# S5 coefficients once per layer, layer 1's tables during layer 0's last projection, lerp and gates with fewer GpSimd passes, three columns opened together

## The chip, the core and the metric

The kernel runs on one core of a Trainium2 chip. The metric is the device time of one execution in microseconds (us). A core has five engines that run side by side, each with its own in-order queue: TensorE (PE, matmuls; PEld is its weight load), VectorE (DVE), ScalarE (ACT), GpSimd (POOL), and SyncE (SP), which here issues the DMAs. Semaphores between the queues carry the dependences.

## The reference

Two pre-norm residual layers on 512 positions of width 2048. The lines that matter here:

```python
h = rms_norm(x);  p = h @ w_in                       # 2048 -> 6,592 columns, then split:
#  A latent attention   B S5   C RWKV-7   D differential attention   and a gate of width 2048
# B (32 groups of 16 channels, one 64-dim complex state per group), coefficients of a layer only:
mag = exp(dt * lr); ab = mag * (cos(dt * li) + i sin(dt * li)); f = (ab - 1) / (lr + i li)
bb = f * (b_re + i b_im);   h_t = ab * h_(t-1) + bb u_t;   y = Re(c h) + d u   # associative scan
# C: token shift of every one of its 13 column tiles
z = z + (z_prev - z) * mu                            # z_prev is z one position earlier
# all four: mix and project
y = concat(A, B, C, D) * silu(gate);  x = x + y @ w_out
```

A final norm follows the last layer.

## The kernel before

**Matmuls.** Everything is fp32 in three passes of a rounded format: each operand is split into a high and a low part, and `three` (L129 records its matmuls) adds low x high, high x low and high x high. `big` runs one output column of 128 features over 512 positions: it streams the weights in chunks of 128x512 (four k tiles of 128). For each chunk SP loads `raw`, ACT casts it to `wh` (L244), DVE subtracts to get `wl` (L245), and PE runs 12 matmuls of 128x512. The ring holds three chunks. A column of the input projection has 16 k tiles, so 48 matmuls. `XH` and `XL` are the two parts of the input times the norm's gain; the norm's row factor `rxr` is multiplied in when a column leaves PSUM (`evacuate`).

**Order.** PE's order is written by hand: `PE.drive` walks the main program `everything` (input projection, output projection, layer by layer) and lets tasks put in their small matmuls at yields given in us of a nominal clock: `recurrent` (RWKV), `others` (S5, both attentions), and the norm. On the other engines a scheduler sets the order at build time, with a head start for the weight chunks. Each engine then runs its list in order, so a DVE instruction that waits for POOL holds up the `wl` behind it.

**The start.** `everything` begins the first two columns of layer 0 together, while x is loaded: per k tile `absorb` makes XH on ACT and XL on DVE (L453), `sum_sq` the square on ACT and the sum `sqs` on POOL (L461). The third column comes after. Up to five columns may wait in PSUM for the norm's factor.

**S5.** `s5_tables` (L329) runs at the head of `others` in both layers: 128x32 tiles of powers of the state factor `pr`, `pi`, then for each of four quarters q a 332-wide tile of coefficients `sm`, written to DRAM, and a rotation table over 64 positions (`tq`, `tr`, `cs`), whose five 128x512 products and sums run on POOL (L434 to L440). `s5_unit` runs 8 times a layer: it loads `sm` (1,328 bytes for each partition), the table and its input, and first makes on POOL `prs` (L794, signed powers) and then, in 8 steps, a copy L809 and a signed copy L810 of the powers in reverse order. DVE forms `CA` (L802 to L804) and `AB` (L811 to L813) from them.

**Lerp and gates.** `z_tile` (L488) evacuates a RWKV column: `zr` on DVE (L494), the difference with the position before on POOL (L496), and z = difference x mu + zr on DVE (L497). A gate column takes a tanh on ACT, a scale and two products on POOL (L1378 to L1380); `mix` (L1388) splits the result into MH and ML for the output projection. The output projection of layer 0 (`out_proj`) runs 16 columns; each result is also absorbed as layer 1's input.

Of the kernel before, what the change touches and what calls it, by code (L numbers as in the profile page):

```python
# [72 lines left out]
ST = {}  # L73
_c = 0
for _n, _w in (("pr", 36), ("pi", 36), ("m8", 4), ("b1", 64), ("b2", 64), ("c1", 64), ("c2", 64)):
    ST[_n] = (_c, _w)
    _c += _w
NST = _c
# [112 lines left out]
def trunk(ctx, tc, io, KT=16, depth=DEPTH):  # L191
# [137 lines left out]
    def s5_tables(pl, l):  # L329
# [23 lines left out]
        pr = pl.tile([128, 9, 32], F32, name="spr", tag="spr")  # L353
        pi = pl.tile([128, 9, 32], F32, name="spi", tag="spi")
        tp = pl.tile([128, 4, 32], F32, name="stp", tag="stp")
        V.memset(pr[:, 0], 1.0)
        V.memset(pi[:, 0], 0.0)
        V.tensor_tensor(out=pr[:, 1], in0=mag, in1=cs, op=ALU.mult)
        V.tensor_tensor(out=pi[:, 1], in0=mag, in1=sn, op=ALU.mult)
        for n in (1, 2, 4):  # L360
            br = pr[:, n:n + 1].to_broadcast([128, n, 32])
            bi = pi[:, n:n + 1].to_broadcast([128, n, 32])
            cmul(pl, V, pr[:, n + 1:2 * n + 1], pi[:, n + 1:2 * n + 1],
                 pr[:, 1:n + 1], pi[:, 1:n + 1], br, bi, tp[:, :n])
        m8 = t32("m8")
# [29 lines left out]
        for q in range(4):  # L395
            g0 = 8 * q
            yield 4.0
            sm = pl.tile([128, 2, NST], F32, name="ssm", tag="ssm", bufs=2)
# [21 lines left out]
            for o, x, y, op in (("b1", 0, 1, ALU.add), ("b2", 1, 0, ALU.subtract)):  # L420
                V.tensor_tensor(out=w2, in0=bc[:, x], in1=frb, op=ALU.mult)
                V.tensor_tensor(out=w, in0=bc[:, y], in1=fib, op=ALU.mult)
                V.tensor_tensor(out=smv(o), in0=halves(w2), in1=halves(w), op=op)
            V.tensor_copy(out=smv("c1"), in_=halves(bc[:, 2]))
            V.tensor_copy(out=smv("c2"), in_=halves(bc[:, 3]))
            SP.dma_start(out=s5sm[l, q], in_=sm.rearrange("p h n -> p (h n)"))
            yield 4.0
# [337 lines left out]
    def s5_unit(sp, l, e, uD, ysD):  # L765
# [17 lines left out]
        def smv(n):  # L783
            o, w = ST[n]
            return sm[:, o:o + w]

        pr = smv("pr").rearrange("p (j g) -> p g j", g=4)
        pi = smv("pi").rearrange("p (j g) -> p g j", g=4)
        b1, b2, c1, c2 = (smv(n).rearrange("p (g c) -> p g c", c=16) for n in ("b1", "b2", "c1", "c2"))
# [904 lines left out]
```

## Time and profile before

| | |
|---|---|
| median of 3 runs | 2083.63 us (2079.5 to 2087.05) |
| profiled execution | 2085.61 us, its span 2083.8 us |
| PE busy | 1977.2 us, 95% |
| DVE busy | 1328.6 us, 64% |
| ACT busy | 816.1 us, 39% |
| POOL busy | 649.7 us, 31% |
| mean granted PE clock | 0.977 of full |

The profile's times count from the first instruction of the span. A row of the timeline has start, duration, engine, line and operation, the tiles out<-in, and in brackets the idle time of the engine before it with what ended that idle time. A row with a count covers several like instructions, and its duration is of them together. An engine's busy time in a window counts stalls inside an instruction too, so an operation that is slowed by its neighbour shows as a longer one.

### The profile page before, as it was taken

To read this page: it belongs to the slowest core of one execution; us is meant where nothing else is said; L and a number is where in the kernel's file an instruction comes from. 1 tells how busy PE (TensorE), PEld (TensorE's weight loads), DVE (VectorE), ACT (ScalarE), POOL (GpSimd) and SP (SyncE) were. 2 spreads that over 40 slices of the span, in tenths; PEclk is the share of its full clock that TensorE was granted. 3 is DMA by queue.
4 is the path that set the end of the run, shared out by engine and by line. 5 is a ranking of instruction groups with operands and counts; after the bars stand their busy time and mean duration, and the time that the engine had idled before them with its cause. 6 is when DMAs were issued, how large, how long until landed. Compare 5 with 4: busy or idle time off the path is not lost.

```text
span 2083.8 us, 31759 instructions
## 1 busy us (share of the span) xinstructions
PE 1977.2 (95%) x10975; PEld 1601.9 (77%) x10975; DVE 1328.6 (64%) x2750; ACT 816.1 (39%) x1680; POOL 649.7 (31%) x837
## 2 busy tenths in 40 slices
PE   7888899999999989999998998999999998999997
PEld 5666677787878778888876786778787886888887
DVE  7987765656756677644477776656684666765332
...
GB/s 193 127 139 128 118 112 132 166 177 167 152 176 123 145 180 149 145 120 176 157 110 159 108 120 125 116 144 202 141 178 197 121 130 180 129 162 119 137 150 119
DMA packets 231922, 303.77 MB, mean 146 GB/s; under 512 B 78160, under 2 KB 102992, under 8 KB 231760
## 3 DMA queue, kind: packets, MB, share of 16 engines
...
q10 hardware_dynamic: 144, 0.17, 0.0%
HBM read 232.08 MB, written 67.21 MB: 144 GB/s over the span
## 4 chain that ended last, share of the span: by engine, by line
PE 62%; DVE 13%; DMA 10%; issue 6%; POOL 6%; ACT 3%; SPq 1%; DVEq 0%; ACTq 0%; POOLq 0%
PE acc L129 46%; PE pb L129 13%; DVE wl L245 3%; PE pb L133 2%; DMA sm<-s5sm 2%; POOL pis L810 1%; DMA raw<-in_w_out_dram 1%; POOL prs L809 1%; DMA raw<-in_w_in_dram 1%; DMA R<-qkD 1%; DVE XL L453 1%; ACT wh L244 1%; DMA qs<-qrD 1%; DMA gt<-ysD 1%; DMA stg<-gD 0%
## 5 line engine op out<-in xcount | busy, mean ns | idle before, releaser
L129 PE MATMUL acc<-XH,wl 128*128 128x512 f32 x1616 | 671.0, 415 | 61.1 <-DVE wl L245 55.4
L129 PE MATMUL acc<-XL,wh 128*128 128x512 f32 x1616 | 641.9, 397 | 5.4 <-DVE XL L453 5.3
L129 PE MATMUL acc<-XH,wh 128*128 128x512 f32 x1616 | 641.4, 397 | 0.0
L244 ACT CAST wh<-raw 128x512 fp32r<-128x512 f32 (+1 forms) x560 | 342.3, 616 | 609.7 <-PE acc L129 437.9
L245 DVE TENSOR_TENSOR wl<-raw,wh 128x512 fp32r<-128x512 f32 (+1 forms) x560 | 415.7, 745 | 239.0 <-ACT wh L244 236.4
L129 PEld LDWEIGHTS acc<-XH,wl 128*128 128x128 f32 x1616 | 310.1, 192 | 150.3 <-DVE wl L245 73.7
L129 PEld LDWEIGHTS acc<-XH,wh 128*128 128x128 f32 x1616 | 309.2, 191 | 68.3
L129 PEld LDWEIGHTS acc<-XL,wh 128*128 128x128 f32 x1616 | 310.2, 192 | 67.0 <-DVE XL L453 9.6
L129 PE MATMUL acc<-MH,wl 128*128 128x512 f32 x448 | 178.5, 398 | 0.0
L129 PE MATMUL acc<-MH,wh 128*128 128x512 f32 x448 | 175.7, 392 | 0.0
L129 PE MATMUL acc<-ML,wh 128*128 128x512 f32 x448 | 174.5, 389 | 0.0
L461 POOL TENSOR_TENSOR sqs<-sqs,sq 128x512 f32<-128x512 f32 (+1 forms) x47 | 60.6, 1289 | 200.1 <-ACT sq L459 199.6
L683 POOL TENSOR_SCALAR tmp<-SV,ec 64x64 f32<-64x64 f32 x112 | 66.2, 593 | 176.0 <-DVE SV L710 94.6
L129 PEld LDWEIGHTS acc<-MH,wh 128*128 128x128 f32 x448 | 84.1, 188 | 19.3
L129 PEld LDWEIGHTS acc<-ML,wh 128*128 128x128 f32 x448 | 84.2, 188 | 17.3
L129 PEld LDWEIGHTS acc<-MH,wl 128*128 128x128 f32 x448 | 84.3, 188 | 16.8
L1378 POOL TENSOR_SCALAR zd<-zd 128x512 f32<-128x512 f32 x32 | 22.5, 703 | 226.3 <-ACT zd L1377 190.3
L1209 POOL TENSOR_TENSOR sr<-ss,cc 128x1 f32<-128x1 f32 x32 | 18.2, 571 | 147.9 <-DVE ss L1207 108.8
L496 POOL TENSOR_TENSOR zd<-zr 128x512 f32<-128x512 f32 x26 | 35.7, 1372 | 82.7 <-DVE zr L494 79.5
L810 POOL TENSOR_SCALAR pis<-sm,cc 128x4 f32<-128x4 f32 x128 | 58.9, 460 | 0.0
L924 ACT ACTIVATE pt<-pb,nb,fc 128x128 f32<-128x128 f32 (+3 forms) x64 | 39.5, 617 | 41.1 <-DVE nb L923 41.1
L626 DVE TENSOR_TENSOR tmp<-X 64x30 f32<-64x30 f32 (+14 forms) x120 | 41.1, 343 | 15.5 <-DMA T<-K 5.5
...
## 6 DMA issues: line engine op xcount, KB each, us to landing
...
raw<-in_w_out_dram SPq DMA_DIRECT2D x128, 256.0 KB, 3.4
...
```

What stands on the lines that cost most here:

```text
L129: return self.nc.tensor.matmul(out, lhsT=lhsT, rhs=rhs, **kw)
L133: return self.nc.tensor.transpose(out, in_, identity)
L244: A.copy(out=wh[:, :n], in_=raw[:, :n])
L245: V.tensor_sub(out=wl[:, :n], in0=raw[:, :n], in1=wh[:, :n])
L453: V.scalar_tensor_tensor(out=XL[:, k], in0=x, scalar=g, in1=XH[:, k], op0=ALU.mult, op1=ALU.subtract)
L461: G.tensor_tensor(out=sqs, in0=sqs, in1=sq, op=ALU.add)
L496: G.tensor_tensor(out=d, in0=zr[:, 0:S], in1=zr[:, 1:], op=ALU.subtract)
L626: V.tensor_tensor(out=t2, in0=X[:, 0:j, j:j + 1].to_broadcast([64, j, n]), in1=X[:, j:j + 1, j + 1:32].to_broadcast([64, j, n]), op=ALU.mult)
L683: G.tensor_scalar(out=T1[T, h], in0=SVs[s][T, c, h], scalar1=ec[T, h, c:c + 1], scalar2=None, op0=ALU.mult)
L810: G.tensor_scalar(out=pis[:, :, i], in0=pi[:, :, 7 - i], scalar1=C("sg"), scalar2=None, op0=ALU.mult)
L924: A.activation(out=pt, in_=ps[:, 0:n], func=AF.Exp, scale=fcol[:, qb:qb + 1], bias=nb, accum_out=sm)
L1378: G.tensor_scalar(out=th, in0=th, scalar1=0.5, scalar2=0.5, op0=ALU.mult, op1=ALU.add)
```

## The change

1. **S5 coefficients.** Once per layer one DVE and 16 small ACT instructions put the signed powers, the reversed ones and m8 into one tile `pw` of 35 values for each group (1,120 values a partition), stored as `s5pw`; b goes to `s5b`, c is read straight from the input. A unit loads three pieces (`pw` 560 bytes, `b` 512 bytes, `c` two times 256 bytes for each partition) in place of `sm`, and its 17 POOL instructions are gone.
2. **Tables.** The copies into `sm` are gone, the five 128x512 passes a quarter move from POOL to DVE, the POOL power is cut into four pieces, and layer 1's tables become a task of layer 0's output projection, which ends only when they are made.
3. **Lerp and gates.** The lerp is zr x (1 - mu) on ACT, then one DVE instruction; a gate needs one DVE and one POOL pass after the tanh, and `mix` multiplies by one half.
4. **Start.** Three columns are opened together, the squares are summed on DVE there, and six columns may wait for the norm.

```diff
-    def s5_tables(pl, l):
+    def s5_tables(pl, l, pace):
...
+        a, b = PW["pr"]
+        V.tensor_scalar(out=pw[:, :, a:b], in0=pr, scalar1=C("sg"), scalar2=-1.0, op0=ALU.mult, op1=ALU.mult)
+        for i in range(8):
+            A.copy(out=pw[:, :, PW["rr"][0] + i], in_=pr[:, :, 7 - i])
+            A.activation(out=pw[:, :, PW["ri"][0] + i], in_=pi[:, :, 7 - i], func=AF.Copy, scale=C("sg"))
...
+        SP.dma_start(out=s5pw[l], in_=pw)
+        yield pace
...
-            for n, x in (("pr", pr), ("pi", pi)):
-                for h in range(2):
-                    V.tensor_copy(out=smv(n)[:, h].rearrange("p (j g) -> p j g", g=4),
-                                  in_=x[:, :, g0 + 4 * h:g0 + 4 * h + 4])
-            V.tensor_copy(out=smv("m8"), in_=m8[:, g0:g0 + 8].rearrange("p (h g) -> p h g", g=4))
...
-            G.tensor_tensor(out=tq, in0=qb, in1=hb, op=ALU.mult)
+            V.tensor_tensor(out=tq, in0=qb, in1=hb, op=ALU.mult)
             V.tensor_scalar(out=tr, in0=tq, scalar1=MAGIC, scalar2=MAGIC, op0=ALU.add, op1=ALU.subtract)
-            G.tensor_tensor(out=tq, in0=tq, in1=tr, op=ALU.subtract)
-            G.tensor_tensor(out=tr, in0=qb, in1=lb, op=ALU.mult)
-            G.tensor_tensor(out=tq, in0=tq, in1=tr, op=ALU.add)
+            V.tensor_tensor(out=tq, in0=tq, in1=tr, op=ALU.subtract)
+            yield pace
+            V.tensor_tensor(out=tr, in0=qb, in1=lb, op=ALU.mult)
+            V.tensor_tensor(out=tq, in0=tq, in1=tr, op=ALU.add)
...
     def z_tile(ps, mu, m1, rxr, out):
-        G.tensor_tensor(out=d, in0=zr[:, 0:S], in1=zr[:, 1:], op=ALU.subtract)
-        V.scalar_tensor_tensor(out=out, in0=d, scalar=mu, in1=zr[:, 1:], op0=ALU.mult, op1=ALU.add)
+        A.activation(out=d, in_=zr[:, 1:], func=AF.Copy, scale=m1)
+        V.scalar_tensor_tensor(out=out, in0=zr[:, 0:S], scalar=mu, in1=d, op0=ALU.mult, op1=ALU.add)
...
-        sm = sp.tile([128, NST], F32, name="sm", tag="sm", bufs=2)
-        SP.dma_start(out=sm, in_=s5sm[l, t, :, hf * NST:(hf + 1) * NST])
+        pw = sp.tile([128, 4, NPW], F32, name="pw", tag="pw", bufs=2)
+        SP.dma_start(out=pw, in_=s5pw[l, :, 4 * e:4 * e + 4])
+        bb = sp.tile([128, 4, 4, 16], F32, name="bb", tag="bb", bufs=2)
+        SP.dma_start(out=bb[:, 0:2].rearrange("p a g c -> p a (g c)"), in_=s5b[l, t, :, hf])
+        SP.dma_start(out=bb[:, 2:4].rearrange("p a g c -> p a (g c)"),
+                     in_=io["s5bc"][l, :, 2:4, 64 * e:64 * e + 64])
...
-        G.tensor_scalar(out=prs, in0=pr, scalar1=C("sg"), scalar2=-1.0, op0=ALU.mult, op1=ALU.mult)
...
-        for i in range(8):
-            G.tensor_copy(out=prs[:, :, i], in_=pr[:, :, 7 - i])
-            G.tensor_scalar(out=pis[:, :, i], in0=pi[:, :, 7 - i], scalar1=C("sg"), scalar2=None, op0=ALU.mult)
-        V.tensor_tensor(out=AB, in0=bj(prs[:, :, 0:8]), in1=bc(b1, 8), op=ALU.mult)
+        V.tensor_tensor(out=AB, in0=bj(rr), in1=bc(b1, 8), op=ALU.mult)
...
-                G.tensor_scalar(out=th, in0=th, scalar1=0.5, scalar2=0.5, op0=ALU.mult, op1=ALU.add)
+                V.scalar_tensor_tensor(out=g, in0=th, scalar=1.0, in1=g, op0=ALU.add, op1=ALU.mult)
                 G.tensor_tensor(out=g, in0=g, in1=y, op=ALU.mult)
-                G.tensor_tensor(out=g, in0=g, in1=th, op=ALU.mult)
...
+            PE.spawn(tables(l + 1), 1)
             for m in range(KT):
...
+            while (l + 1, "tab") not in PE.done:
+                yield False
             PE.spawn(norm_task(l + 1, sqs), -1)
...
-        begun = [acc(), acc()]
+        begun = [acc(), acc(), pb()]
...
-                    absorb(st, k0 + j, x[:, j], pvts[0], sqs)
-            yield from big([io["w_in"][0, i] for i in range(2)], KT, XH, XL, begun, st, (8, 4), inputs)
+                    absorb(st, k0 + j, x[:, j], pvts[0], sqs, V)
+            yield from big([io["w_in"][0, i] for i in range(3)], KT, XH, XL, begun, st, (9, 6), inputs)
```

Three places show how the engines' lists move. First DVE around the first S5 units of layer 0, before; `prs` and `pis` come from POOL, `sm` from a DMA, `m` is the scan's factor.

```order
L803 TENSOR_TENSOR W<-sm 128x576 [waits DMAHW6_49]
L846 COPY m_1994<-sm 128x256 [waits DMAHW3_49]
L802 TENSOR_TENSOR CA<-prs,sm 128x576 [waits DMAHW2_49,DMAHW3_49,DVE_49,Pool_49]
L847 MEMSET m_1994 128x4 [waits DVE_49]
L804 TENSOR_TENSOR CA<-CA,W 128x576 [waits DVE_49]
L245 TENSOR_TENSOR wl<-raw,wh 128x512 [waits DMAHW1_49,Activation_49]
L811 TENSOR_TENSOR AB<-prs_1690,sm 128x512 [waits Pool_49]
L812 TENSOR_TENSOR W<-pis,sm 128x4x128 [waits Pool_49]
L803 TENSOR_TENSOR W<-sm 128x576 [waits DMAHW2_49,DVE_49]
L813 TENSOR_TENSOR AB<-AB,W 128x512 [waits DVE_49]
L245 TENSOR_TENSOR wl<-raw,wh 128x512 [waits DMAHW5_49,Activation_49]
```

The same place now; `pw` and `bb` are what the three loads bring.

```order
L836 COPY m_1820<-pw 128x256 [waits DMAHW7_49]
L801 TENSOR_TENSOR AB<-pw,bb 128x512 [waits DMAHW0_49]
L837 MEMSET m_1820 128x4 [waits DVE_49]
L243 TENSOR_TENSOR wl<-raw,wh 128x512 [waits DMAHW3_49,Activation_49]
L796 TENSOR_TENSOR CA<-pw,bb 128x576 [waits DMAHW4_49,DMAHW6_49,DMAHW2_49,DMAHW1_49]
L797 TENSOR_TENSOR W<-pw,bb 128x576
L802 TENSOR_TENSOR W<-pw,bb 128x4x128
L801 TENSOR_TENSOR AB<-pw,bb 128x512 [waits DMAHW6_49,DMAHW5_49]
L798 TENSOR_TENSOR CA<-CA,W 128x576 [waits DVE_49]
L243 TENSOR_TENSOR wl<-raw,wh 128x512 [waits Activation_49]
```

The waits for POOL are gone, and the products wait for DMAs alone. Second, SP's list of DMAs at the same place, before.

```order
L776 DMA sm<-s5sm 128x332
L778 DMA tab<-s5tab 128x2x256 [waits PE_49]
L242 DMA raw<-in_w_in_dram 128x512 [waits DMAHW0_49,DVE_49]
L781 DMA U_1678<-uD_348 128x256 [waits DMAHW1_49]
L776 DMA sm<-s5sm 128x332 [waits DMAHW2_49]
L778 DMA tab<-s5tab 128x2x256 [waits DMAHW3_49,Pool_49]
```

And now:

```order
L774 DMA pw<-s5pw 128x140
L776 DMA bb<-s5b 128x128 [waits DMAHW0_49,PE_49]
L777 DMA bb<-in_s5bc_dram 128x2x64 [waits DMAHW1_49]
L240 DMA raw<-in_w_in_dram 128x512 [waits DMAHW2_49,DVE_49]
L780 DMA tab<-s5tab 128x2x256 [waits DMAHW3_49]
L783 DMA U_1613<-uD_422 128x256 [waits DMAHW4_49]
L774 DMA pw<-s5pw 128x140 [waits DMAHW5_49]
L776 DMA bb<-s5b 128x128 [waits DMAHW6_49]
L777 DMA bb<-in_s5bc_dram 128x2x64 [waits DMAHW7_49]
```

Each unit has two more DMAs ahead of the weight chunks that follow. Third, DVE in the first columns of layer 0's output projection, before; `xo` is a finished column.

```order
L1457 TENSOR_TENSOR xo<-acc,xo 128x512 [waits DMAHW3_49,PE_49]
L245 TENSOR_TENSOR wl<-raw,wh 128x512 [waits DMAHW3_49,Activation_49]
L453 SCALAR_TENSOR_TENSOR XL<-xo,pvt,XH 128x512 [waits Activation_49]
L1457 TENSOR_TENSOR xo<-acc,xo 128x512 [waits DMAHW7_49,DMAHW5_49,PE_49]
L245 TENSOR_TENSOR wl<-raw,wh 128x512 [waits DMAHW4_49,Activation_49]
L453 SCALAR_TENSOR_TENSOR XL<-xo,pvt,XH 128x512 [waits Activation_49]
L245 TENSOR_TENSOR wl<-raw,wh 128x512 [waits DMAHW6_49,Activation_49]
```

And now, with the rotation table of layer 1 (`tq`, `tr`, `cs`):

```order
L243 TENSOR_TENSOR wl<-raw,wh 128x512 [waits DMAHW2_49,Activation_49]
L451 SCALAR_TENSOR_TENSOR XL<-xo,pvt,XH 128x512 [waits Activation_49]
L441 TENSOR_SCALAR cs_9854<-cs_9854,cc 128x512 [waits Activation_49]
L431 TENSOR_TENSOR tq<-cc,sthi 128x512 [waits DVE_49,Activation_49]
L441 TENSOR_SCALAR cs_10060<-cs_10060,cc 128x512 [waits Activation_49]
L431 TENSOR_TENSOR tq<-cc,sthi 128x512 [waits DVE_49,Activation_49]
L243 TENSOR_TENSOR wl<-raw,wh 128x512 [waits DMAHW3_49,Activation_49]
L432 TENSOR_SCALAR tr<-tq 128x512 [waits DVE_49]
L298 TENSOR_SCALAR cs_9854<-cs_9854 128x512 [waits Activation_49]
L298 TENSOR_SCALAR cs_10060<-cs_10060 128x512 [waits Activation_49]
L432 TENSOR_SCALAR tr<-tq 128x512 [waits DVE_49]
L243 TENSOR_TENSOR wl<-raw,wh 128x512 [waits DMAHW6_49,Activation_49]
```

In this piece four table instructions and more stand between two `wl`; before, they stood in layer 1's input projection. From the first table instruction to the last, this list has 26 `wl`.

## Rows read from the trace of the kernel before

**Rows 1.** The page's busy times, shares of the span and instruction counts.

```profile
PE 1977.2 (95%) x10975; PEld 1601.9 (77%) x10975; DVE 1328.6 (64%) x2750; ACT 816.1 (39%) x1680; POOL 649.7 (31%) x837
```

**Rows 2.** PE's waits: engine, line, what it waited for; us, times, longest.

```profile
PE acc L129 <- DVE wl L245: 55.4, 33, 5.6
PE pb L129 <- DVE BK L586: 6.9, 3, 5.9
...
PE acc L129 <- DVE zr L494: 5.1, 1, 5.1
```

**Rows 3.** Busy us (and instructions) of each engine by window, PEclk, DMA share, GB/s.

```profile
6.00:42.00 36.00, 27.35 (x103) 17.98 (x102) 33.05 (x29) 24.09 (x43) 22.77 (x19) 1.00 0.59 209
...
60.00:180.00 120.00, 100.22 (x441) 78.86 (x440) 105.34 (x204) 44.57 (x73) 69.21 (x82) 0.90 0.44 139
220.00:310.00 90.00, 80.50 (x515) 64.89 (x513) 65.28 (x142) 29.75 (x69) 41.36 (x91) 0.89 0.39 116
...
920.00:1060.00 140.00, 140.00 (x617) 115.06 (x617) 62.12 (x94) 53.11 (x86) 25.97 (x25) 1.00 0.51 157
1080.00:1160.00 80.00, 63.84 (x260) 49.46 (x260) 66.48 (x124) 28.36 (x45) 58.93 (x71) 0.87 0.38 128
1240.00:1360.00 120.00, 110.17 (x847) 87.53 (x846) 77.81 (x167) 42.82 (x107) 63.51 (x148) 0.97 0.40 118
```

**Rows 4.** Timeline of the start, and the first matmul of the third column.

```profile
6.99 0.50 PE L129 MATMUL acc<-XH,wl 128*128 128x512 f32 x1 [0.42 <-ACT XH L452]
...
15.54 1.30 POOL L461 TENSOR_TENSOR sqs<-sqs,sq 128x512 f32<-128x512 f32 x1 [0.44 <-ACT sq L459]
15.57 5.87 DVE L453 SCALAR_TENSOR_TENSOR XL<-x,pvt,XH 128x512 fp32r<-128x512 f32 x4
...
23.66 0.74 DVE L453 SCALAR_TENSOR_TENSOR XL<-x,pvt,XH 128x512 fp32r<-128x512 f32 x1
...
41.17 0.39 PE L129 MATMUL pb<-XH,wl 128*128 128x512 f32 x1
```

**Rows 5.** Line L245 over the whole run: ns of one, min/median/max.

```profile
L245 DVE TENSOR_TENSOR wl<-raw,wh x560: 411/691/1781, 6.1 to 2016.2; 128x512 fp32r<-128x512 f32 x184, 128x256 fp32r<-128x256 f32 x3
```

**Rows 6.** Timeline of DVE in the tables of layer 0.

```profile
92.21 0.41 DVE L435 TENSOR_SCALAR tr<-tq 128x512 f32<-128x512 f32 x1
...
92.94 0.28 DVE L423 TENSOR_TENSOR ssm<-sw,sw 128x128 f32<-128x128 f32 x1
```

**Rows 7.** POOL and ACT groups by line: busy us, mean ns, idle before and its releasers.

```profile
L810 POOL TENSOR_SCALAR pis<-sm,cc 128x4 f32<-128x4 f32 x128 | 58.9, 460 | 0.0
...
L809 POOL COPY prs<-sm 128x4 f32<-128x4 f32 x128 | 36.3, 284 | 0.0
L496 POOL TENSOR_TENSOR zd<-zr 128x512 f32<-128x512 f32 x26 | 35.7, 1372 | 82.7 <-DVE zr L494 79.5 <-DVE sfi L384 3.2
...
L434 POOL TENSOR_TENSOR tq<-cc,sthi 128x512 f32<-128x512 f32 x8 | 13.2, 1653 | 4.7 <-ACT cs L298 3.7 <-DVE sthi L393 1.0
```

**Rows 8.** Timeline of two S5 units of layer 0.

```profile
165.30 0.96 POOL L794 TENSOR_SCALAR prs<-sm,cc 128x36 f32<-128x36 f32 x1
...
171.88 0.69 DVE L811 TENSOR_TENSOR AB<-prs,sm 128x512 f32<-128x512 f32 x1 [2.02 <-POOL prs L809]
...
174.38 1.66 DVE L245 TENSOR_TENSOR wl<-raw,wh 128x512 fp32r<-128x512 f32 x1
...
176.10 0.79 PE L129 MATMUL acc<-XH,wl 128*128 128x512 f32 x1 [5.59 <-DVE wl L245]
...
242.41 0.69 DVE L811 TENSOR_TENSOR AB<-prs,sm 128x512 f32<-128x512 f32 x1 [2.89 <-POOL prs L809]
```

**Rows 9.** Timeline of the first S5 units of layer 1.

```profile
1138.33 0.76 DVE L803 TENSOR_TENSOR W<-sm 128x576 f32<-128x576 f32 x1 [3.58 <-DMA sm<-s5sm]
...
1149.98 2.28 PE L129 MATMUL pb<-Q,BK 64*128 64x128 f32 x9 [5.94 <-DVE BK L586]
```

**Rows 10.** DMA issues: count, size of one, median us from issue to landing.

```profile
sm<-s5sm SPq DMA_DIRECT2D x16, 166.0 KB, 4.0
```

More of the change, by code (lines that the diff above doesn't have):

```diff
@@ L70 @@
 NPV = _c
[L73 to L78, printed above, removed]
+PW = {"pr": (0, 9), "pi": (9, 18), "rr": (18, 26), "ri": (26, 34), "m8": (34, 35)}
+NPW = 35
 Y = {
@@ L340, in exp_ @@
         def exp_(out, x):
-            G.tensor_tensor(out=out, in0=C("e"), in1=x, op=ALU.pow)
+            for a in range(0, 32, 8):
+                G.tensor_tensor(out=out[:, a:a + 8], in0=C("e", a, a + 8), in1=x[:, a:a + 8], op=ALU.pow)
             V.tensor_scalar(out=t2, in0=x, scalar1=delta, scalar2=1.0, op0=ALU.mult, op1=ALU.add)
@@ L352, in s5_tables @@
         sincos(th, sn, cs)
[L353 to L359, printed above, removed]
-        for n in (1, 2, 4):
[L361 to L365, printed above, removed]
+        yield pace
+        pr = pl.tile([128, 32, 9], F32, name="spr", tag="spr")
+        pw = pl.tile([128, 32, NPW], F32, name="spw", tag="spw")
+        pi = pw[:, :, PW["pi"][0]:PW["pi"][1]]
+        tp = pl.tile([128, 32, 4], F32, name="stp", tag="stp")
+        V.memset(pr[:, :, 0], 1.0)
+        V.memset(pi[:, :, 0], 0.0)
+        V.tensor_tensor(out=pr[:, :, 1], in0=mag, in1=cs, op=ALU.mult)
+        V.tensor_tensor(out=pi[:, :, 1], in0=mag, in1=sn, op=ALU.mult)
+        for n in (1, 2, 4):
+            br = pr[:, :, n:n + 1].to_broadcast([128, 32, n])
+            bi = pi[:, :, n:n + 1].to_broadcast([128, 32, n])
+            cmul(pl, V, pr[:, :, n + 1:2 * n + 1], pi[:, :, n + 1:2 * n + 1],
+                 pr[:, :, 1:n + 1], pi[:, :, 1:n + 1], br, bi, tp[:, :, :n])
+        yield pace
+        a, b = PW["pr"]
[3 more added lines that the diff above has]
+            A.activation(out=pw[:, :, PW["ri"][0] + i], in_=pi[:, :, 7 - i], func=AF.Copy, scale=C("sg"))
+        m8 = pw[:, :, PW["m8"][0]]
         V.tensor_tensor(out=m8, in0=mag, in1=mag, op=ALU.mult)
@@ L418, in halves @@
                 return x.rearrange("p (h g) c -> p h (g c)", h=2)
-            for o, x, y, op in (("b1", 0, 1, ALU.add), ("b2", 1, 0, ALU.subtract)):
+            for o, x, y, op in ((0, 0, 1, ALU.add), (1, 1, 0, ALU.subtract)):
                 V.tensor_tensor(out=w2, in0=bc[:, x], in1=frb, op=ALU.mult)
                 V.tensor_tensor(out=w, in0=bc[:, y], in1=fib, op=ALU.mult)
[L423 to L427, printed above, removed]
+                V.tensor_tensor(out=sb[:, :, o], in0=halves(w2), in1=halves(w), op=op)
+            SP.dma_start(out=s5b[l, q], in_=sb)
+            yield pace
             qb = C("qidx").unsqueeze(1).to_broadcast([128, 8, 64])
@@ L460, in sum_sq @@
         if not first:
-            G.tensor_tensor(out=sqs, in0=sqs, in1=sq, op=ALU.add)
+            eng.tensor_tensor(out=sqs, in0=sqs, in1=sq, op=ALU.add)
     def colsum(sqs):
@@ L486, in norm_col, with z_tile @@
         res += [col, rows_of(lp, col, name + "r")]
-    def z_tile(ps, mu, rxr, out):
+    def z_tile(ps, mu, m1, rxr, out):
         zr = zp.tile([128, S + 1], F32, name="zr", tag="zr", bufs=1)
@@ L781, in s5_unit @@
         SP.dma_start(out=U8.rearrange("p g q -> p (g q)"), in_=uD[t, :, gq])
[L783 to L789, printed above, removed]
+        pr, pi, rr, ri, m8c = (pw[:, :, a:b] for a, b in (PW[n] for n in ("pr", "pi", "rr", "ri", "m8")))
+        b1, b2, c1, c2 = (bb[:, j] for j in range(4))
         CA, W = t3("CA", 9), t3("W", 9)
-        prs = sp.tile([128, 4, 9], F32, name="prs", tag="prs", bufs=4)
-        pis = sp.tile([128, 4, 9], F32, name="pis", tag="pis", bufs=2)
-        G.tensor_scalar(out=prs, in0=pr, scalar1=C("sg"), scalar2=-1.0, op0=ALU.mult, op1=ALU.mult)
         def bj(x):
@@ L1241, in tables @@
         with sub("tab", l) as st:
-            yield from s5_tables(st, l)
-        if l == 0:
-            with sub("rope", l) as st:
-                yield from rope_tables(st)
+            yield from s5_tables(st, l, 3.0 if l == 0 else 6.0)
         PE.done.add((l, "tab"))
@@ L1261, in __init__ @@
             self.pvt = pvts[l]
-            self.dv = cp.tile([128, 16], F32, name="dv", tag="dv")
+            self.dv = cp.tile([128, 29], F32, name="dv", tag="dv")
             for j, (n, m, a) in enumerate((("w0", 0.5, 0.0), ("a0", 0.5, 0.0), ("k_a", -1.0, 1.0),
@@ L1267, in __init__ @@
                                 scalar2=a, op0=ALU.mult, op1=ALU.add)
+            o = PV["mu"][0]
+            V.tensor_scalar(out=self.dv[:, 16:29], in0=self.pvt[:, o:o + 13], scalar1=-1.0, scalar2=1.0,
+                            op0=ALU.mult, op1=ALU.add)
         def P(self, n, j):
-            DV = {"w0h": 0, "a0h": 4, "k_a1": 8, "bgh": 12}
+            DV = {"w0h": 0, "a0h": 4, "k_a1": 8, "bgh": 12, "mu1": 16}
             if n in DV:
@@ L1315, in others @@
             l, P = self.l, self.P
-            yield from tables(l)
+            if l == 0:
+                yield from tables(l)
+                with sub("rope", l) as st:
+                    yield from rope_tables(st)
             yield from self.need(("u", 3), ("tab",))
@@ L1436, in in_proj @@
                 pend.append((n, t, ps))
-                while len(pend) == 5 and l not in rx:
+                while len(pend) == 6 and l not in rx:
                     yield False
```

54 lines of the change are left out of this document (26 added, 28 removed).

## The prediction, made before the changed kernel ran

> **What bounds the kernel now.** I read the page's busy times first, then PE's waits, then a table of windows, then the timeline inside the windows that lose time. PE is busy 95% of the span and no other engine comes near [rows 1], so a change elsewhere can gain only where PE waits or its clock falls. PE's waits name one releaser above all: DVE's `wl`, 55.4 us in 33 waits; BK adds 6.9, `zr` 5.1 [rows 2]. The windows say where. In 920 to 1060 PE is full: 617 matmuls in 140.00 us, 0.227 us each, so a column of 48 takes 10.9 us and a chunk of 12 takes 2.72. In five other windows PE idles: 8.65 us of 6 to 42, 19.78 of 60 to 180, 9.50 of 220 to 310, 16.16 of 1080 to 1160, 9.83 of 1240 to 1360, and in the middle three the granted clock is 0.90, 0.89 and 0.87 of full [rows 3], a mean over stretches at 2.4 and at 1.2 GHz. In 60 to 180 DVE is busy 105.34 of 120 us and POOL 69.21; in 1080 to 1160 they are at 66.48 and 58.93 of 80: the S5 tables run there. So the kernel is bound by PE, and in these windows by DVE, partly through POOL.
>
> **A, the start.** The first matmul of the two columns stands at 6.99 and the first of the third at 41.17 [rows 4]: 34.2 us for 96 matmuls that need 21.8. The third column then ends at 52.1. Three columns together are 144 matmuls, 32.7 us, so 39.7 is the earliest end and 12.4 us the most to gain. Per k tile PE needs 9 x 0.227 = 2.04 us. DVE made four XL in 5.87 us beside POOL's sum of squares (1.30 us), 1.47 each, but one in 0.74 without it [rows 4]. Now it also does the sum (0.69, the median of L245, the same kind of instruction [rows 5]) and 3/4 of a `wl` (0.52): 1.95 us at the lone price, just under PE. If XL stays at 1.47, it is 2.68, the columns end at 49.9, and 2.2 us are gained. ACT has 12 us left of the 36 [rows 3] for four more casts. Between 2 and 12 I take 8, nearer to the lone price, since POOL has nothing left there that slows DVE.
>
> **B, layer 0's tables and first S5 units (60 to 180).** Lost are 19.78 us of idle and, by the clock, a tenth of the 100.22 busy: 30 us; PE's own need is 90. DVE's need, from its 105.34 busy us: the moved passes add 20 x 0.69 = 13.8 (the dropped copies I count at nothing; they can only help). POOL loses five passes in each of four quarters at 1.65 [rows 7], 33 at most and some 30; seven `zd` at 1.37, 10; and two units' lists of one 0.96 [rows 8] and 8 x (0.460 + 0.284), 6.9 each, 14: 54 us of its 69. XL lost 0.73 us beside a POOL pass of 1.30, so 54 us of POOL gone give DVE back between nothing and 30. DVE thus needs 89 to 119 against PE's 90, plainly still at its limit, but fluid. One stall is named: DVE waited 2.02 us for the list of L809, the `wl` behind it then took 1.66, and PE idled 5.59 [rows 8]; with the slower clock after it some 8. That one goes, since the new list of DVE has no wait for POOL there. I take 14 of 30; the ends are 0 and 25.
>
> The rows show a DVE pass losing 0.73 us beside a POOL pass of 1.30. The Trainium skill (SBUF — State Buffer, Who interferes with whom) calls it an exclusive lock: of a DVE instruction with two SBUF inputs and a GpSimd one that reads SBUF, the second waits until the first ends. The trace agrees in kind (0.74 against 1.47), not in amount; by the lock the relief would be nearer 54 than 30, which is the first rival.
>
> **C, layer 0's other S5 units (220 to 310).** Idle 9.50 and 80.50 x 0.11 = 8.9 by the clock, 18 us. DVE's wait for L809 was 2.89 here [rows 8]. Four units' lists, 28 us, are two thirds of POOL's 41.36. I take 8; the ends are 0, where the unit waits for its loads instead, and 14.
>
> **D, layer 1's beginning (1080 to 1160).** Idle 16.16 and 63.84 x 0.13 = 8.3, 24 us. The tables leave altogether, some 33 us of DVE's 66.48 (under F) and 30 of POOL's 58.93; the S5 lists, 14, and `zd` go too. The longest wait, 5.94 for BK [rows 9], came behind POOL's S5 list. Both of PE's releasers there fall below half of the time. I take 19; the ends are 10 and 24.
>
> **E, layer 1's later S5 units (1240 to 1360).** Idle 9.83 and 110.17 x 0.03 = 3.3. Most waits are RWKV's own. I take 3; the ends are 0 and 8.
>
> **F, what is added.** Layer 1's tables now stand in layer 0's output projection: 26 chunks of `wl` from the first table row to the last in the new DVE order, 70.7 us of PE. DVE's own need there is 62.12 / 140 of it, 31.4. The tables: 20 passes at 0.69, 16 of one input at 0.41, 24 of 128x128 at 0.28 [rows 5, 6], together 27, and some 65 of 128x32, between nothing and 0.28; I take 0.1 by size, 6. That is 64 us in 70.7, with three chunks (8 us) in the ring. It fits, but the rows bunch. I take -4; the ends are 0 and -44 (last rival). At nothing I cost: 26 lerp passes on ACT, which is busy 44.57 of 120 where they fall; 32 more gate passes on DVE, busy 62.12 of 140 there, against 64 POOL passes less; 16 small ACT instructions a layer (if uncovered 16 x 0.28 = 4.5); 32 more DMAs from SP, covered unless the unit waits for them (third rival). One more column ahead of the norm delays RWKV's chain by 10.9 us of PE, which PE fills with columns.
>
> **Sum.** 8 + 14 + 8 + 19 + 3 - 4 = 48. The profiled execution took 2085.61, so 2037.6; the median of before is 1.98 below it, so 2036.
>
> **Rivals.** First, the relief is whole: a POOL pass blocked DVE for its full length. Then DVE in 60 to 180 needs 119 - 54 = 65 of 90, B is 25, D 24, C 11: 67 in all, 2017. For it: `wl` at 1.66 and up to 1.78 where 0.69 is the rule [rows 5, 8]. Against it: XL lost 0.73 of 1.30. The rule is the lock of the Trainium skill's page SBUF — State Buffer.
>
> Second, DVE stays the bound of layer 0: passes moved from POOL to DVE lie on the engine that PE already waits for. B falls to 4, A to 2, F to -10: 26 in all, 2058. For it: 105.34 of 120 and the 13.8 added, the 1.95 of 2.04 at the start. Against it: a good part of DVE's busy time is POOL's doing.
>
> Third, the S5 units wait for their loads. DVE already idled 3.58 us for `sm` [rows 9], which lands in 4.0 [rows 10]; now three loads come one after the other, and the scan factor and `AB` stand in DVE's list ahead of a `wl`. The gains that are POOL's list (C 8, E 3, 6 of B, 6 of D) go: 25 in all, 2059. Against it: the loads have two buffers, so can come a unit ahead. The Trainium skill (DMA: Bandwidth & Descriptors, Specifications) says that transfers under 512 bytes are handled as read-modify-write; c comes in pieces of 256 bytes, and by this the third rival gains. No run here shows a load of that size alone.
>
> Last, slower: the tables choke layer 0's output projection. If every DVE pass in those 26 chunks is slowed as XL was (1.47 for 0.74), DVE needs 64 x 1.98 = 127 us, less 70.7 and the ring's 8 leaves 48 idle, and the clock at 0.87 over the 119 us takes 15 more: 63 in place of 4, so 48 - 59 = -11, 2095. It starts above a slowing of 79 / 64 = 1.23, and turns the total only near the full factor. Against it: POOL is busy 25.97 of 140 there.
>
> **How the numbers follow.** Chances: forecast 0.52, whole relief 0.09, DVE the bound 0.19, loads 0.13, slower 0.07. 0.3%, 6 us, is about what a measurement can tell from no change. All but the last case are faster by far more; weak mixtures of the last leave 0.04 for the same: faster 0.90, same 0.04, slower 0.06. The likeliest case alone spans 2024 to 2048; the range reaches to the second and third rivals and beyond the first, 2010 to 2062, leaving out some 0.15.
>
> **What would show it.** A: the fourth column's first matmul before 45, XL near 0.74. B to D: no DVE wait for POOL ahead of a product of S5; PE idle in 60 to 180 near 10, in layer 1's first 80 us under 5, the clock there above 0.95. F: PE nearly full in layer 0's output projection, DVE up by some 33 us. Wrong it would be if DVE's busy time in layer 0's first 180 us grew, if S5's products waited for `pw` or `bb` over 2 us, or if PE idled over 15 us in the output projection.

## The result, and the profile after

The changed kernel took 2018.86 us (2017.32 to 2023.51, 4 runs) against 2084.39 for the one before on the same chip: 0.9686 of it, 95% interval 0.9668 to 0.9704, or 65.5 us less. Forecast were 2036 us and 2010 to 2062. The busy times and PE's waits of the changed kernel's page, to be read against [rows 1, 2]:

```profile
PE 1953.9 (97%) x10975; PEld 1592.7 (79%) x10975; DVE 1308.3 (65%) x2785; ACT 839.3 (42%) x1736; POOL 377.4 (19%) x432
```

```profile
PE acc L126 <- DVE wl L243: 14.8, 12, 3.5
PE acc L126 <- DVE zr L492: 10.7, 1, 10.7
PE pb L126 <- DVE BK L584: 3.9, 1, 3.9
PE acc L126 <- DVE xo L1452: 3.3, 2, 2.1
```

POOL's busy time fell by 272 us, and PE's waits for `wl` from 55.4 to 14.8 us; the one wait for `zr` rose from 5.1 to 10.7. The same windows as in [rows 3], columns as there:

```profile
6.00:42.00 36.00, 34.65 (x143) 26.25 (x142) 30.28 (x55) 26.87 (x49) 4.03 (x7) 1.00 0.71 258
60.00:180.00 120.00, 105.41 (x480) 85.33 (x479) 99.30 (x201) 56.49 (x99) 19.17 (x22) 0.91 0.47 144
...
920.00:1060.00 140.00, 139.32 (x620) 114.97 (x619) 85.31 (x141) 59.59 (x100) 23.05 (x23) 1.00 0.55 174
1080.00:1160.00 80.00, 80.00 (x417) 65.36 (x416) 55.21 (x77) 26.24 (x46) 18.98 (x17) 1.00 0.39 116
1240.00:1360.00 120.00, 119.37 (x851) 94.99 (x851) 81.19 (x165) 49.78 (x112) 31.62 (x47) 1.00 0.50 150
```

Layer 1's beginning has no idle left and the full clock; layer 0's 60 to 180 still has 14.6 us of idle and 0.91. A fixed window holds other work in the two kernels, so from here on the span is cut by work: the projections' matmuls are counted in groups of 48, in PE's order, and a stage runs from the start of one group to that of another (A from the start of the span). Times in us from the profiled executions, each worked out from the start times of two matmuls:

| stage, groups | before | after | forecast gain | measured |
|---|---|---|---|---|
| A, 0 to 4: the start | 63.9 | 54.0 | 8 | 9.9 |
| B, 4 to 12: tables, first S5 units | 133.7 | 123.7 | 14 | 10.0 |
| C, 12 to 22: other S5 units of layer 0 | 182.5 | 169.5 | 8 | 13.0 |
| 22 to 56 | 540.7 | 540.6 | 0 | 0.1 |
| F, 56 to 70: last gates, output projection | 155.0 | 161.2 | -4 | -6.2 |
| D, 70 to 78: layer 1's beginning | 129.4 | 103.3 | 19 | 26.1 |
| E, 78 to 88: S5 and RWKV of layer 1 | 175.5 | 163.3 | 3 | 12.2 |
| 88 to the end | 703.1 | 702.4 | 0 | 0.7 |

The cut is exact for the projections; the small matmuls between them can move. With three columns opened, 8, 16 and 16 fewer of these stand in A, B and C, and 40 more in 22 to 56; with two columns (e5 below) every stage holds as many as before.

In the changed kernel's timeline the S5 products follow each other without a wait for POOL, and `wl` stands at its lone time:

```profile
137.12 0.69 DVE L801 TENSOR_TENSOR AB<-pw,bb 128x512 f32<-128x512 f32 x1
137.74 0.68 DVE L243 TENSOR_TENSOR wl<-raw,wh 128x512 fp32r<-128x512 f32 x1
```

### The profile page after: what moved, and what is told of

Read it like the earlier page. It is cut to its first block, busy times and chain, and to the rows that moved or that the text cites. A ratio compares the mean times of both kernels' runs of the same rounds, so it can differ in the third digit from the quotient of the medians.

```text
span 2017.9 us, 31460 instructions
## 1 busy us (share of the span) xinstructions
PE 1953.9 (97%) x10975; PEld 1592.7 (79%) x10975; DVE 1308.3 (65%) x2785; ACT 839.3 (42%) x1736; POOL 377.4 (19%) x432
## 4 chain that ended last, share of the span: by engine, by line
PE 77%; DMA 8%; DVE 7%; issue 2%; ACT 2%; SPq 1%; POOL 1%; DVEq 0%; ACTq 0%
PE acc L126 58%; PE pb L126 17%; PE pb L130 2%; DVE wl L243 2%; DMA stg<-gD 1%; DMA raw<-in_w_out_dram 1%; DMA raw<-in_w_in_dram 1%; DMA raw<-qkD 1%; DMA R<-qkD 1%; SPq L821 1%; DMA T<-K 0%; DMA qs<-qrD 0%; DVE tmp L624 0%; DMA raw<-in_w_uv_dram 0%; DVE X L626 0%
## 5 line engine op out<-in xcount | busy, mean ns | idle before, releaser
L126 PE MATMUL acc<-XH,wl 128*128 128x512 f32 x1600 | 656.2, 410 | 25.2 <-DVE wl L243 14.2
L126 PE MATMUL acc<-XL,wh 128*128 128x512 f32 x1600 | 629.2, 393 | 1.1 <-DVE XL L451 1.1
L126 PE MATMUL acc<-XH,wh 128*128 128x512 f32 x1600 | 629.6, 393 | 0.0
L243 DVE TENSOR_TENSOR wl<-raw,wh 128x512 fp32r<-128x512 f32 (+1 forms) x560 | 397.0, 712 | 234.0 <-ACT wh L242 231.6
L126 PEld LDWEIGHTS acc<-XH,wl 128*128 128x128 f32 x1600 | 303.3, 190 | 103.8 <-DVE wl L243 20.3
L126 PEld LDWEIGHTS acc<-XL,wh 128*128 128x128 f32 x1600 | 303.7, 190 | 60.2 <-DVE XL L451 2.7
L126 PE MATMUL acc<-MH,wh 128*128 128x512 f32 x448 | 175.5, 392 | 0.0
L1372 POOL TENSOR_TENSOR stg<-stg,zr 128x512 f32<-128x512 f32 x32 | 43.4, 1355 | 219.6 <-DVE stg L1371 140.4
L459 POOL TENSOR_TENSOR sqs<-sqs,sq 128x512 f32<-128x512 f32 (+1 forms) x32 | 42.0, 1311 | 187.2 <-ACT sq L457 187.1
L911 DVE TENSOR_TENSOR pb<-pb,cc 128x128 f32<-128x128 f32 x96 | 26.5, 294 | 36.6 <-PE pb L126 35.1
L912 DVE TENSOR_REDUCE mx<-pb 128x1 f32<-128x128 f32 (+3 forms) x96 | 45.9, 478 | 0.5
```

Of the source, the lines that this page charges most:

```text
L126: return self.nc.tensor.matmul(out, lhsT=lhsT, rhs=rhs, **kw)
L243: V.tensor_sub(out=wl[:, :n], in0=raw[:, :n], in1=wh[:, :n])
L459: eng.tensor_tensor(out=sqs, in0=sqs, in1=sq, op=ALU.add)
L911: V.tensor_tensor(out=ps[:, qb * 128:n], in0=ps[:, qb * 128:n], in1=C("neg"), op=ALU.add)
L912: V.tensor_reduce(out=mx, in_=ps[:, 0:n], axis=AX.X, op=ALU.max)
L1372: G.tensor_tensor(out=g, in0=g, in1=y, op=ALU.mult)
```

## The experiments

The stages of every kernel, in us as above:

| kernel | A | B | C | F | D | E | time / before, 95% |
|---|---|---|---|---|---|---|---|
| changed | 54.0 | 123.7 | 169.5 | 161.2 | 103.3 | 163.3 | 0.9686 (0.9668 to 0.9704) |
| e1 list | 53.9 | 126.5 | 170.5 | 162.2 | 103.2 | 170.5 | 0.9736 (0.9713 to 0.9759) |
| e2 dead list | 53.8 | 124.6 | 176.3 | 161.6 | 103.2 | 165.5 | 0.9718 (0.9697 to 0.9740) |
| e3 tables late | 53.9 | 124.2 | 169.1 | 154.5 | 112.2 | 163.5 | 0.9696 (0.9671 to 0.9721) |
| e4 sum on POOL | 57.6 | 124.6 | 169.7 | 161.3 | 103.2 | 164.0 | 0.9700 (0.9680 to 0.9720) |
| e5 two columns | 54.7 | 122.0 | 167.1 | 157.8 | 103.2 | 163.5 | 0.9636 (0.9610 to 0.9663) |
| e6 lerp on POOL | 53.9 | 127.0 | 170.1 | 161.2 | 103.2 | 164.0 | 0.9694 (0.9671 to 0.9717) |
| e7 passes on POOL | 54.0 | 118.2 | 167.7 | 171.8 | 103.2 | 164.0 | 0.9690 (0.9666 to 0.9714) |
| e11 S5 undone | 53.9 | 117.4 | 172.7 | 154.9 | 135.0 | 171.3 | 0.9803 (0.9776 to 0.9830) |
| e12 S5 and lerp undone | 53.9 | 123.9 | 174.2 | 154.9 | 135.1 | 169.9 | 0.9860 (0.9835 to 0.9884) |
| b1 before, sum on DVE | 54.6 | 131.7 | 182.9 | 155.0 | 128.9 | 178.5 | 0.9957 (0.9940 to 0.9973) |
| e13 put together | 54.5 | 118.9 | 166.5 | 157.7 | 103.2 | 163.4 | 0.9625 (0.9599 to 0.9651) |
| e14 the same, lerp on DVE | 54.9 | 123.5 | 171.3 | 157.7 | 103.2 | 166.3 | 0.9642 (0.9614 to 0.9669) |

A ratio is against the kernel before on the same chip. The intervals of e2 (just), e3, e4, e6 and e7 overlap the changed kernel's: their totals are not told apart from it, only single stages are. Each stage is read from one execution, which can lie some us off its kernel's median (e14's by 6.4, e11's by 4.1). D repeats within a tenth where no edit touches it (103.2), but the last part of the span, behind group 88, which no edit is aimed at, takes 698.8 to 703.1, and a stage that follows a changed one can shift by some us: a difference of 1 or 2 us in a stage says little.

**e1, the list back, and waited for.** In each unit:

```diff
+        G.tensor_scalar(out=prs, in0=pr, scalar1=1.0, scalar2=1.0, op0=ALU.mult, op1=ALU.mult)
...
+        for i in range(8):
+            G.tensor_copy(out=prr[:, :, i], in_=rr[:, :, i])
+            G.tensor_scalar(out=pis[:, :, i], in0=ri[:, :, i], scalar1=1.0, scalar2=None, op0=ALU.mult)
...
-        V.tensor_tensor(out=AB, in0=bj(rr), in1=bc(b1, 8), op=ALU.mult)
+        V.tensor_tensor(out=AB, in0=bj(prr[:, :, 0:8]), in1=bc(b1, 8), op=ALU.mult)
...
```

> The changed kernel, but every S5 unit makes its 17 POOL instructions again (copies of what the new tile already holds) and DVE's products read those copies. The wait theory (DVE stood in line behind this list, and the weight chunk stood behind DVE): about 25 to 35 us come back, 2044 to 2054, with DVE idle 2 to 3 us before AB, and PE idle again in the S5 stretches of both layers. The contention theory (POOL's accesses slowed DVE's passes) expects the same total here, and is told apart by the next kernel.

2031.24 us: some 10 to 12 came back, not 25 to 35, and 7 of them in E. DVE's group for AB and, in E, one of its waits and what it does to RWKV's small matmuls:

```profile
L808 DVE TENSOR_TENSOR AB<-prs,bb 128x512 f32<-128x512 f32 x16 | 11.0, 689 | 9.3 <-POOL prs L794 7.3 <-DMA bb<-in_s5bc_dram 1.5 <-PE pb L126 0.4
```

```profile
1294.17 0.69 DVE L808 TENSOR_TENSOR AB<-prs,bb 128x512 f32<-128x512 f32 x1 [2.33 <-POOL prs L794]
...
1296.62 0.45 PE L126 MATMUL pb<-tmp,NM 64*64 64x64 f32 x8 [1.39 <-DVE tmp L672]
```

The longest waits are as forecast, but there are few of them: 7.3 us for `prs` over 16 units (the kernel before had 20.6, in 9 waits). D did not move at all (103.2), so the list alone was not what held layer 1's beginning.

**e2, the same list, read by nobody.** The edit is e1's POOL instructions alone; DVE's products stay as they are.

> The changed kernel with the same 17 POOL instructions in every S5 unit, written to tiles that nobody reads; DVE's products read the loaded tile as in the changed kernel. Wait theory: 2019 to 2025, since nobody waits for the list. Contention theory: most of the loss of the kernel with the list comes back, 2035 or more, with wl and S5 products at 1.2 us and above in those stretches.

2027.32 us, between the two theories. DVE's mean `wl` over the run, in the changed kernel and in this one (busy, mean ns, idle before):

```profile
L243 DVE TENSOR_TENSOR wl<-raw,wh 128x512 fp32r<-128x512 f32 (+1 forms) x560 | 397.0, 712 | 234.0 <-ACT wh L242 231.6
```

```profile
L243 DVE TENSOR_TENSOR wl<-raw,wh 128x512 fp32r<-128x512 f32 (+1 forms) x560 | 396.9, 712 | 234.1 <-ACT wh L242 231.8
```

The list does not slow DVE's `wl`: 712 ns both times. It can delay what stands behind it in POOL's own queue, for which DVE waits in its turn. In C, POOL's clearing of `T` came right behind the list, the DMAs that fill `T` behind that:

```profile
263.32 0.52 POOL L826 MEMSET T<- 128x512 f32 x1
264.57 0.42 DVE L841 TENSOR_TENSOR v<-v,sw 128x256 f32<-128x256 f32 x1 [1.84 <-POOL sw L840]
...
272.08 0.76 DVE L804 TENSOR_TENSOR W<-pw,bb 128x576 f32<-128x576 f32 x1 [2.30 <-DMA T<-K]
```

PE then stood 3.2 us, and the loss, 7 us in C, follows there. So a third theory: not the awaited result and not the access, but POOL's queue in front of something that is needed. From this run it is read at one place, not tried; and it is not the length of the queue alone, for e1 has the same list, clears `T` at 263.39, and loses 1.0 in C. What differs is the order of the lists around it; no run changed that alone. The kernel before shows the same kind of wait in E, larger (under E below).

**e3, layer 1's tables at its own head.** The task is not spawned in the output projection; `others` runs `tables(l)` in both layers, at the pace of layer 0.

> The changed kernel, but layer 1's tables stand again at the head of layer 1's S5 task and not in layer 0's output projection. If it is the place of the tables that cleared layer 1's beginning: 2032 to 2040 (26 us lost there, 7 got back in the output projection), PE idle some 12 us in the first 80 us of layer 1. Rival, that the tables without POOL passes and without the S5 list would have fitted there: 2011 to 2021, the output projection's 7 us back and nothing lost.

2022.24 us, just above the rival's range. D lost 8.9 and F got 6.7 back. The window of D in this kernel:

```profile
1080.00:1160.00 80.00, 75.76 (x370) 61.03 (x369) 62.26 (x93) 25.81 (x44) 15.03 (x16) 0.94 0.45 135
```

4.2 us of idle, where the kernel before had 16.16: the tables without POOL passes and without the list almost fit there.

**e4 and e5, the start.** e4 gives `absorb` the POOL engine again, with three columns; e5 opens two, with the sum on DVE.

> The changed kernel, but the sum of squares of the start is on POOL again, with three columns opened together. Contention theory: XL takes 1.4 us and more again in place of 0.75, DVE needs about 2.0 us per k tile against PE's 2.04 and wl passes are slowed too; the start ends 3 to 10 us later, 2022 to 2029. Rival, that the third column alone made the gain and covers the slower XL: within 2 us, 2017 to 2021.

> The changed kernel, but only two columns are opened together, the sum of squares stays on DVE. The prediction's step A: with two columns PE needs 1.37 us per k tile and DVE 0.75 + 0.69 + 0.35 = 1.8, so the start is bound by DVE and ends some 7 us later, and the layer keeps the loss: 2024 to 2028. Rival, that the relief of XL made the gain: the two columns end 8 us earlier than before and 2 us at most are lost, 2017 to 2021.

**b1, the kernel before with the sum on DVE.**

> The kernel before with one edit: the start's sum of squares on DVE in place of POOL; still two columns together. If the relief of XL makes the start's gain (XL 0.75 in place of 1.46), the two columns end near 32 in place of 41, 9 us, and the whole is 9 us faster or a little less: 2074 to 2080. If three columns are needed for it, 2081 to 2086.

e4 2023.19, e5 2011.19, b1 2076.55 against 2085.02. XL of the start in e4, e5 and b1:

```profile
L451 DVE SCALAR_TENSOR_TENSOR XL<-x,pvt,XH 128x512 fp32r<-128x512 f32 x16 | 20.0, 1298 | 0.9 <-ACT XH L450 0.9
```

```profile
L451 DVE SCALAR_TENSOR_TENSOR XL<-x,pvt,XH 128x512 fp32r<-128x512 f32 x16 | 11.5, 746 | 0.5 <-ACT XH L450 0.4
```

```profile
L453 DVE SCALAR_TENSOR_TENSOR XL<-x,pvt,XH 128x512 fp32r<-128x512 f32 x16 | 11.5, 747 | 0.6 <-ACT XH L452 0.6
```

The sum on DVE with two columns makes A 54.7, three columns with the sum on POOL 57.6, both 54.0, neither 63.9. Either edit brings most of it; the third column adds 0.7. b1 alone kept its 9 us to the end. And with two columns the rest of layer 0 is shorter (B 122.0, C 167.1, F 157.8): e5 is faster than the changed kernel, its interval lies just below. Why is not shown; PE's wait for `zr` is 6.0 there, and 0.8 us, in place of 3.3, for `xo` in the output projection.

**e6 and e7, lerp or table passes back on POOL.** e6 restores the POOL subtraction in `z_tile`; e7 makes the five passes with `G.tensor_tensor`.

> The changed kernel, but the lerp's first pass is the difference on POOL again in place of ACT's product. Theory that each part alone is worth little while POOL is otherwise nearly empty: within 3 us of the changed kernel. Theory that the new 10.7 us wait of PE for zr comes from DVE's second lerp pass waiting for ACT, which is in line with table loads for sine and exponential: this wait falls to under 6 us, 2012 to 2018. Rival, that POOL passes beside wl are dear: 2024 or more.

> The changed kernel, but the five 128x512 passes of each quarter of the S5 tables are on POOL again. Contention theory: a pass of 1.6 us on POOL slows DVE by more than the 0.69 it takes on DVE itself, so the first 180 us lose and the output projection too, 2024 to 2034. Rival, that DVE was the bound there and is relieved of 28 us in all: 2008 to 2017.

e6 2024.64: B is 3.3 longer, and PE's wait for `zr` is 12.9, not less. So ACT's pass is not what makes this wait. e7 2023.50, and no wait for `zr`; its windows of 60 to 180 and 920 to 1060:

```profile
60.00:180.00 120.00, 110.13 (x504) 86.97 (x503) 106.53 (x188) 54.97 (x100) 52.52 (x44) 0.96 0.49 148
...
920.00:1060.00 140.00, 133.42 (x588) 108.66 (x588) 82.66 (x116) 57.86 (x95) 38.17 (x35) 1.00 0.55 170
```

Layer 0's tables are better off on POOL (B 118.2 for 123.7), layer 1's, inside the output projection, on DVE (F 161.2 for 171.8). It is not that DVE has room there. Where the tables are densest, it is full in both kernels; first the changed one, then e7, and e7's waits of PE in the output projection:

```profile
898.00:915.00 17.00, 13.44 (x55) 9.86 (x54) 16.09 (x64) 8.41 (x22) 3.40 (x4) 0.99 0.35 107
```

```profile
898.00:915.00 17.00, 11.04 (x36) 8.03 (x37) 17.00 (x46) 6.28 (x16) 10.00 (x8) 0.84 0.42 140
```

```profile
PE acc L126 <- DVE xo L1452: 8.8, 4, 4.4
```

The two stretches hold nearly, not quite, the same work. With POOL busy 10.00 of the 17 us, DVE got through 46 instructions, with POOL at 3.40 through 64: DVE's passes are longer in e7 (1.1 to 1.8 us for several whose quick time is 0.28 to 0.74).

**e11 and e12, several undone.** e11 is e1, e3 and e7 together; e12 is e11 and e6.

> The changed kernel with three things undone together: the S5 units' list on POOL with DVE waiting for it, the table passes on POOL, and layer 1's tables at the head of layer 1. If the parts add up (12 for the list, 3 for the place, and what the passes alone cost, some 5), 2036 to 2042. If they hold each other up, each part being covered as long as the others leave POOL and DVE room, the sum is far more: 2050 to 2065, and the stalls in layer 1's beginning come back, over 15 us of PE idle there.

> The changed kernel with four things undone together: the S5 list on POOL with DVE waiting, the table passes on POOL, layer 1's tables at layer 1's head, and the lerp's difference on POOL. The kernel with the first three undone took 2048. If the lerp adds only what it cost alone, 6 us: 2052 to 2057. If list and lerp passes stand in each other's way on POOL, as in the kernel before where the lerp's pass took up to 3.6 us behind the list, 2060 to 2074, with 6 us or more lost between columns 12 and 22.

e11 2048.13, e12 2056.81. In D, the list alone costs 0, the passes alone 0 (the tables are not there), the place alone 8.9; the three together cost 31.7, more than the whole forecast for D. e11's window of D and PE's waits from 1070 to 1160:

```profile
1080.00:1160.00 80.00, 64.50 (x287) 50.48 (x287) 49.55 (x73) 28.39 (x47) 36.99 (x73) 0.87 0.37 113
```

```profile
PE acc L126 <- DVE wl L243: 8.3, 3, 5.3
PE pb L126 <- DVE BK L584: 7.2, 1, 7.2
```

The kernel before had the same two waits in 1080 to 1160:

```profile
PE acc L129 <- DVE wl L245: 10.1, 6, 3.2
PE pb L129 <- DVE BK L586: 5.9, 1, 5.9
```

But in e11 DVE is busy only 49.55 of the 80 us. It stands in line: for ACT, which had the tables' sines in its list, for a late load, for the list, and for POOL work behind it:

```profile
1094.15 0.43 DVE L537 TENSOR_SCALAR tmp<-tmp 128x512 f32<-128x512 f32 x1 [3.00 <-ACT tmp L536]
...
1102.55 0.37 DVE L843 COPY m<-pw 128x256 f32<-128x256 f32 x1 [3.42 <-DMA pw<-s5pw]
...
1107.33 0.69 DVE L808 TENSOR_TENSOR AB<-prs,bb 128x512 f32<-128x512 f32 x1 [1.57 <-POOL prs L794]
...
1120.42 0.55 DVE L576 TENSOR_SCALAR tmp<-tmp,pvt,dv 128x512 f32<-128x512 f32 x1 [2.31 <-POOL E L530]
```

The load was late because SP issued it late. Its queue had waited for DVE's `cs`, to store a table (L443), and `pw` of layer 1's first unit stood behind that store:

```profile
SPq L443 <- DVE cs L298: 8.4, 2, 7.3
```

```profile
1096.96 0.58 SPq L774 DMA_DIRECT2D pw<-s5pw  x1
```

So this part comes from the tables' place; layer 1's first list begins only when the load has landed, at 1102.54. No two of the three were undone without the third, so whether a pair would fill the stage is not known. At 135.0 us the stage is longer than in the kernel before (129.4).

**e13 and e14, put together.** Two columns, and in the tables:

```diff
-            V.tensor_tensor(out=tq, in0=qb, in1=hb, op=ALU.mult)
+            (G if l == 0 else V).tensor_tensor(out=tq, in0=qb, in1=hb, op=ALU.mult)
...
```

The other four passes are changed alike.

> A version put together from the runs: the changed kernel with two columns opened together (2011 alone) and layer 0's table passes on POOL, layer 1's on DVE. The passes on POOL gave 5 us by column 12 of layer 0 and lost 8 in the output projection, where these stay on DVE. If both gains add: 2003 to 2008. Rival, that both relieve the same stall around column 8 of layer 0: 2009 to 2014.

> The same version, with the lerp's product by (1 - mu) on DVE (one input, 0.41 us) in place of ACT. Theory that DVE's wait for ACT, which is in line with table loads, makes the wait of PE for zr (6 us with two columns): this wait goes, 3 to 6 us faster than the kernel without it. Rival, that DVE is full there and each 0.41 more (26 passes, 10.7 us) is paid: 2 to 6 us slower than it.

e13 2007.67 (2006.05 to 2009.7): 0.9625, below the changed kernel's interval and the shortest of all, not told apart from e5. In 60 to 180 PE has no wait for `zr`, though over the run its waits for `wl` are 31.1 us, against 14.8 in the changed kernel:

```profile
60.00:180.00 120.00, 110.73 (x525) 86.43 (x524) 111.01 (x168) 54.19 (x93) 48.93 (x42) 0.97 0.48 151
```

e14 2010.51: no gain from taking ACT out of the lerp; the interval overlaps e13's. B and C are 4.6 and 4.8 longer in its profile, but the profiled execution (2016.86) was the longest of its four, so these two say little.

## Why the prediction came out as it did

The direction, the places and the range held; the size was short by 17 us. By the terms of its sum:

- **A** was right in size, 8 for 9.9, and its DVE time per k tile held (XL 0.748 and the sum 0.687 us; the fourth column's first matmul at 43.1, before the 45 named). But it counted the third column and the relief of XL as one gain. They are two ways to the same one.
- **B**, 14 for 10.0. The named stall behind L809 went. The prediction's second rival is true in kind in this stage: the moved passes went onto the engine that PE waits for. PE stood 10.72 us for `zr`, which stood in DVE's list behind passes of the tables, one of which waited for ACT's sine:

```profile
107.01 0.98 DVE L298 TENSOR_SCALAR cs<-cs 128x512 f32<-128x512 f32 x1 [1.74 <-ACT cs L297]
...
110.33 0.69 DVE L492 TENSOR_TENSOR zr<-acc,rxr 128x512 f32<-128x512 f32 x1
...
111.08 0.79 PE L126 MATMUL acc<-XH,wl 128*128 128x512 f32 x1 [10.72 <-DVE zr L492]
```

With these passes on POOL the wait is gone (e7, e13).
- **F**, -4 for -6.2. Counted by work, over the same 684 matmuls, DVE rose by 35 us, for the 33 forecast (the changed kernel, then the kernel before):

```profile
888.00:1049.00 161.00, 156.76 (x685) 128.00 (x684) 108.29 (x223) 72.49 (x127) 37.92 (x32) 0.99 0.54 170
```

```profile
921.00:1076.00 155.00, 155.00 (x686) 127.44 (x685) 72.81 (x140) 60.28 (x99) 36.65 (x28) 1.00 0.48 150
```

PE idled 4.2 us there, most of it before 920, where the window of 920 to 1060 does not show it: 3.3 us for `xo`, which stood in DVE's list between the tables' instructions. So the rows bunched, as the prediction feared, and it cost little; the slower rival, with every DVE pass slowed, did not come.
- **D** was mis-sized, 19 with an upper end of 24 for 26.1. The step held that the tables leave; the runs show that their place alone is 8.9 of it (e3), and that the stage fills when place, passes and list come together (e11), while list or passes alone cost it nothing. With the three undone together 31.7 comes back, 5.6 more than the change gained, so the other parts of the change cost something there or the lists fall differently.
- **E** was the worst, 3 with an upper end of 8 for 12.2. The step that failed is "Most waits are RWKV's own". In the kernel before, the longest of them, 3.49 us for RWKV's `tmp`, hung on S5. POOL's product `sw`, which DVE needed, stood behind the next unit's list, and that list behind the load of its `sm`; DVE stood 6.16 us for it, and ACT copied RWKV's `tmp` (L651) only behind copies of what DVE then made:

```profile
1285.52 0.33 POOL L794 TENSOR_SCALAR prs<-sm,cc 128x36 f32<-128x36 f32 x1 [5.53 <-DMA sm<-s5sm]
...
1289.02 0.73 POOL L843 TENSOR_TENSOR sw<-sw,tab 128x256 f32<-128x256 f32 x1
...
1289.78 0.42 DVE L844 TENSOR_TENSOR v<-v,sw 128x256 f32<-128x256 f32 x1 [6.16 <-POOL sw L843]
...
1292.63 1.18 ACT L651 COPY tmp<-pb 32x512 f32<-32x512 f32 x2
...
1293.26 3.43 PE L129 MATMUL pb<-NM,tmp 32*32 32x32 f32 x64 [3.49 <-ACT tmp L651]
```

The group of 48 in which this stands took 28.3 us and takes 20.5 now, 7.8 of the 12.2. Over the run DVE waited 14.5 us for this product, in 7 waits, before, and under 1 us in the changed kernel. With the list back (e1) 7.2 us of E return, with waits of PE for RWKV's tiles, but only 1.7 of them in this group: there the list stands behind `sw`. So undoing the list in the changed kernel does not bring back all that it cost in the kernel before.
- **C**, 8 for 13.0. The list's wait explains 1.0 of it alone (e1), the unread list 6.8 (e2), the four undone parts 4.7 (e12). What makes up the other 8, and a similar part of B (e11 is faster in B than the changed kernel, b1 slower by 8.0), was not separated: left in e12 are the third and the sixth column, the gates, the cut POOL power, the dropped copies, the new loads and the order of the lists. It is not the third column's shift of small matmuls: with two columns and the same work as before, e5 gains 15.4 in C and 11.7 in B.

In all, undoing four parts (e12) brings back some 36 of the 65.5 us; A, which it keeps, is 9.9; the rest, some 19, was not separated.

The first rival, a relief of POOL's full length, came nearest in time (2017) but not in kind. A sum over all DVE instructions in the trace, of each one's time above the quick fifth of its kind (the same operation and shapes), falls from some 160 us to some 96, while POOL lost 272 us busy. e7's 40 passes put back 28 of it for 58 us of POOL, about half a us for each us, as the prediction took from XL; the list in e1 puts back under 1 for 100. The Trainium skill (SBUF — State Buffer, Who interferes with whom) calls the ports that the two engines share an exclusive lock; the wide passes fit that in kind. Of the narrow ones it was POOL's that stretched, up to 6.3 us for one of 0.23 (e2). The third rival, loads, did not come: in the changed kernel DVE's longest wait for a unit's load is 2.0 us, once, for `bb`.
